# Start addresses of the tiles: a wider constant below, a small pool above

## The chip, the cores and the metric

The kernel runs on one core of a Trainium2 chip. The metric is the device time of one execution in microseconds; the kernel before has a median of 2309.77 us in three runs (2309.41 to 2312.48).

## The reference

One layer of a transformer-like trunk in float32, for 512 tokens of width 2048. The input `x` is normalised (RMS), scaled and shifted by values that a conditioning vector `c` gives through a 2048 x 12288 matrix, and projected to 7168 columns. Half of the heads (8 of width 128) run a gated linear recurrence, half (8 of width 128) run stick-breaking attention with normalised queries and keys. Their normalised outputs are concatenated, projected back to 2048 and added to `x` with a gate. Then a second normalisation of the same kind, and a feed-forward part of width 5632, `silu(gate) * up`, whose output is added with another gate:

```python
h = rms_norm(x, norm1_g[layer]) * (1.0 + sc1) + sh1
proj = h @ w_in[layer]
...
mixed = jnp.concatenate([o_hg, o_sb], axis=-1).astype(x.dtype) @ w_out[layer]
x = x + g1 * mixed

h = rms_norm(x, norm2_g[layer]) * (1.0 + sc2) + sh2
gate, up = jnp.split(h @ w_ffn_in[layer], 2, axis=-1)
x = x + g2 * ((jax.nn.silu(gate) * up) @ w_ffn_out[layer])
```

## The kernel before, in words

**Numbers.** The big products are made of matmuls in `float32r` (fp32r): each float32 operand is split into a rounded part and its remainder, and three matmuls (`hi*hi`, `hi*lo`, `lo*hi`) add up in PSUM. `three` (L227), `product` (L908) and `multiply` issue them. `split` (L212) makes the two parts of a loaded weight block: ScalarE (ACT) casts it to `hi` (L220), VectorE (DVE) subtracts to get `lo` (L221). A few small products (attention scores, transposes) are plain float32, which TensorE (PE) runs in two passes.

**Stages, in order of time.** First projection of the 1024 columns of the recurrence's values (to about 101 us; 16 blocks of rows, 24 matmuls of 512 columns each, while the rows of the conditioning matrix are read and multiplied on DVE, L180). Projections of the eight attention heads (to 445 us; 192 matmuls of 384 columns a head), with the attention of the heads before beside them. Projections of the eight recurrent heads (to 770 us; 144 matmuls of 512 columns a head), with their recurrence beside them. Output projection (to 945 us; 48 matmuls of 512 columns for each of 15 blocks, and the last block in two halves of 256). The first two blocks of the feed-forward part, 384 matmuls of 256 columns (to 1020 us). Then the loop over blocks `f` = 2 to 43 (to about 1850 us): seven products of a Strassen-like scheme on half-blocks, of 24 matmuls with 256 columns each, 168 in an `f`. In it the stationary operand (the weights) comes from `split`, the moving one is a fixed half-block of the activations, opA, opB, opC or opD. Last the output of the feed-forward part (to the end): 12 units of seven products, over 4 or 3 pairs of rows; a product has 6 matmuls of 512 columns for each pair of rows. The pairs of all units add up to 44.

The order of the instructions is written out ahead: a small clock in the kernel (`Clock`) hands out side work at planned times, and the tile framework orders the rest by priority. It inserts all waits. All large DMAs are issued from SP.

**Where tiles lie.** Each partition of the on-chip memory (SBUF) is filled from two ends. Pools with `side="right"` hang from the upper end downwards; the others stand on the lower end upwards, in the order in which they are opened; a tile takes a slot rounded up to 32 bytes. Below the first pool lie 384 bytes of the framework's own (256 of DMA scratch and four constants of 32), and above the uppermost tile 32 bytes of the 229,376 remain unused.

The lowest pool, `const`, holds small tiles for the whole run. Its slots are `cond` 8192, `small` 640, `ones` 512, `epsb` 32, `lead` 32, `mod` 384, `gain1` 64, `gain2` 64, `rcol` 32, `ident2` 512, `qkg` 32, `ba` 64, `lbt` 32, `oml` 32, `lbs` 32: 10,656 bytes. With the 384 below, the pool `wp` above it starts at byte 11,040, which is 86 x 128 + 32. Nearly all other tiles on the left have sizes that are multiples of 128, so the weights' raw blocks and their parts `hi` and `lo` (pool `wp`, L212), the activations `hhi`, `hlo`, `ohi`, `olo` (pool `hp`, L256) and opA to opD all start 32 bytes past a multiple of 128. `cond`, at byte 384, and `ones` start at one. On the right, everything ends at byte 229,344, which is 1791 x 128 + 96, and the tiles there have sizes that are multiples of 128: `xo` and `x1`, `O`, `forms`, `fhi`, `sg`, `up`, `ffS` and the spare parts `hi2` and `lo2` start 96 bytes past one. In the feed-forward loop every fourth call of `split` puts its two parts into `hi2` and `lo2` (`spare_here`, L1095) in place of `wp`; they show as `ff_2hi`, `ff_2lo` in the profile, the others as `ff_1h`, `ff_1l`. In the last stage the spare parts lie in a free piece of `opsB`, on the left.

`epsb` (L158) is a constant bias that one kind of instruction reads (L940, twice). `lead` (L160) takes two partial sums at the very start (L291, L293).

Of the kernel before, what the change touches and what calls it, by code (L numbers as in the profile page):

```python
# [10 lines left out]
F32 = mybir.dt.float32  # L11
# [6 lines left out]
P = 128  # L18
# [17 lines left out]
EPS = 1e-6  # L36
# [93 lines left out]
def trunk(ctx, tc, a):  # L130
    nc = tc.nc
    V, S, G = nc.vector, nc.scalar, nc.gpsimd
# [2 lines left out]

    const = ctx.enter_context(tc.tile_pool(name="const", bufs=1))
    wp = ctx.enter_context(tc.tile_pool(name="wp", bufs=3))
    xctx = ctx.enter_context(ExitStack())
    xop = xctx.enter_context(tc.tile_pool(name="xop", bufs=1, side="right"))
    hp = ctx.enter_context(tc.tile_pool(name="hp", bufs=1))  # L140
# [14 lines left out]
    ones = const.tile([P, P], F32, name="ones")  # L155
    G.memset(ones, 1.0)
    one = ones[:, 0:1]
    epsb = const.tile([P, 1], F32, name="epsb")  # L158
    G.memset(epsb, EPS)
    lead = const.tile([P, 2], F32, name="lead")  # L160
    left = [KT] * 6
    mod = const.tile([P, 96], F32, name="mod")
    gain1 = const.tile([P, KT], F32, name="gain1")
# [1179 lines left out]
```

## Time and profile before

| | |
|---|---|
| median of three runs | 2309.77 us |
| the profiled execution | 2309.45 us, of which the span is 2307.6 us |
| PE, DVE, ACT busy | 2253.1, 1919.5, 1160.1 us |
| mean granted TensorE clock | 0.995 of 2.4 GHz |
| DMA | 437.69 MB, 190 GB/s on the mean |

The span reaches from the first to the last instruction; the profiled execution's own time has 1.85 us more around it. Busy PE includes matmuls that overlap, so PE's share does not tell how fast they follow each other; the distance between the starts of two of them does.

### The profile page before, as it was taken

Reading aid. Unit: us, or ns where it says so; the run is one execution under the profiler, and the core shown is the slowest. Engines: PE = TensorE matmul, PEld = TensorE weight load, DVE = VectorE, ACT = ScalarE, POOL = GpSimd, SP = SyncE. Lnnn points to the kernel's source line nnn. Section 1 sums busy time; section 2 is a strip of 40 time slices with the busy share of each in tenths; the row PEclk is TensorE's granted clock in tenths of the full one; section 3 lists DMA queues with packets and bytes.
Section 4 is the critical chain, followed back from the end, with each engine's and each line's share of the span. In section 5 each row is a group of like instructions: output and inputs, shape, how many; then the busy total and the mean of one; then the engine's idle time right before and its main releaser. Section 6 shows DMA issues by size and latency. Waiting matters only on the chain.

```text
span 2307.6 us, 35720 instructions
## 1 busy us (share of the span) xinstructions
PE 2253.1 (98%) x14171; PEld 2049.8 (89%) x14171; DVE 1919.5 (83%) x2570; ACT 1160.1 (50%) x2011; POOL 10.7 (0%) x25
## 2 busy tenths in 40 slices
PE   8999899999999999989999999999999999999998
PEld 6899799888888788989999999999999978878776
DVE  8887779999887864699899988888888777888888
ACT  4326666565656422654445444454545545454443
POOL 0000000000000000000000000000000000000000
PEclk9999999999999999999999999999999999999999
DMA  9886446843322486336555534454544486654553
GB/s 368 314 319 225 166 153 230 305 170 126 110 92 76 155 294 209 111 114 238 206 203 197 209 133 165 142 174 142 174 142 157 177 343 237 219 178 142 183 204 87
DMA packets 114978, 437.69 MB, mean 190 GB/s; under 512 B 9822, under 2 KB 58236, under 8 KB 76796
## 3 DMA queue, kind: packets, MB, share of 16 engines
q1 hardware_dynamic: 114812, 435.42, 53.0%
q8 instruction: 111, 1.82, 0.3%
q14 instruction: 55, 0.45, 0.1%
HBM read 386.61 MB, written 48.77 MB: 189 GB/s over the span
## 4 chain that ended last, share of the span: by engine, by line
PE 79%; DVE 11%; DMA 4%; ACT 3%; issue 3%; SPq 0%; DVEq 0%; ACTq 0%
PE ffA L93 17%; PE ffC L93 9%; PE foA L93 8%; PE sbp L93 8%; PE wo L93 7%; PE ffB L93 4%; PE foC L93 4%; PE st L93 4%; PE hgf L93 4%; PE hgq L93 3%; PE hgg L93 3%; PE foB L93 1%; DVE ada L180 1%; PE l L93 1%; DMA opd<-fhi 1%
## 5 line engine op out<-in xcount | busy, mean ns | idle before, releaser
L180 DVE SCALAR_TENSOR_TENSOR ada<-ada,cond 128x2048 f32<-128x2048 f32 x95 | 216.9, 2286 | 49.0 <-DMA ada<-in_w_ada 49.0
L93 PE MATMUL ffA<-opD,ff_3h 128*128 128x256 f32 x512 | 93.6, 283 | 0.8 <-ACT u L1008 0.8
L93 PE MATMUL ffA<-opB,ff_6h 128*128 128x256 f32 x512 | 93.6, 283 | 0.2 <-ACT a L1008 0.2
L93 PE MATMUL ffC<-opB,ff_7h 128*128 128x256 f32 x512 | 93.5, 283 | 0.0
L93 PE MATMUL ffC<-opC,ff_4h 128*128 128x256 f32 x496 | 90.8, 284 | 0.4 <-ACT c L1008 0.3
L93 PE MATMUL ffB<-opA,ff_2h 128*128 128x256 f32 x496 | 91.3, 284 | 0.0
L93 PE MATMUL ffA<-opC,ff_5h 128*128 128x256 f32 x496 | 90.6, 283 | 0.0
L93 PE MATMUL ffA<-opA,ff_1h 128*128 128x256 f32 x496 | 90.6, 283 | 0.0
L1082 ACT CAST fhi<-forms 128x512 fp32r<-128x512 f32 (+1 forms) x63 | 43.6, 692 | 90.6 <-DMA opd<-fhi 74.1
L93 PEld LDWEIGHTS ffA<-opD,ff_3h 128*128 128x128 f32 x512 | 79.8, 192 | 1.0 <-ACT u L1008 1.0
L93 PEld LDWEIGHTS ffA<-opB,ff_6h 128*128 128x128 f32 x512 | 79.7, 192 | 0.4 <-ACT a L1008 0.4
L93 PEld LDWEIGHTS ffC<-opB,ff_7h 128*128 128x128 f32 x512 | 79.8, 192 | 0.0
L93 PEld LDWEIGHTS ffC<-opC,ff_4h 128*128 128x128 f32 x496 | 77.2, 192 | 0.8 <-ACT c L1008 0.8
L93 PEld LDWEIGHTS ffB<-opA,ff_2h 128*128 128x128 f32 x496 | 77.7, 193 | 0.1
L93 PEld LDWEIGHTS ffA<-opC,ff_5h 128*128 128x128 f32 x496 | 77.3, 192 | 0.0
L93 PEld LDWEIGHTS ffA<-opA,ff_1h 128*128 128x128 f32 x496 | 77.3, 192 | 0.0
L1083 DVE TENSOR_TENSOR forms<-forms,fhi 128x512 fp32r<-128x512 f32 (+1 forms) x63 | 49.0, 778 | 31.0 <-ACT fhi L1082 30.6
L93 PE MATMUL ffA<-opD,ff_3l 128*128 128x256 f32 x256 | 72.5, 283 | 0.0
L93 PE MATMUL ffC<-opB,ff_7l 128*128 128x256 f32 x256 | 72.4, 283 | 0.0
L93 PE MATMUL ffA<-opB,ff_6l 128*128 128x256 f32 x256 | 72.4, 283 | 0.0
L93 PE MATMUL ffB<-opA,ff_2l 128*128 128x256 f32 x248 | 70.3, 284 | 0.0
L93 PE MATMUL ffA<-opA,ff_1l 128*128 128x256 f32 x248 | 70.2, 283 | 0.0
(1644 smaller groups left out, 7759.3 us busy)
## 6 DMA issues: line engine op xcount, KB each, us to landing
ada<-in_w_ada SPq DMA_DIRECT2D x95, 1024.0 KB, 5.0
wfo<-in_w_fo SPq DMA_DIRECT2D x16, 1024.0 KB, 6.0
yraw<-in_w_fo SPq DMA_DIRECT2D x16, 1024.0 KB, 5.1
fix<-in_w_fix SPq DMA_DIRECT2D x14, 1024.0 KB, 5.7
opsA<-opd SPq DMA_DIRECT2D x12, 1024.0 KB, 4.9
opd<-forms SPq DMA_DIRECT2D x44, 256.0 KB, 3.7
opd<-fhi SPq DMA_DIRECT2D x42, 256.0 KB, 4.2
opd<-forms SPq DMA_DIRECT2D x22, 384.0 KB, 6.7
```

Source lines behind the costliest of these rows:

```text
L93: self.engine.matmul(out, lhsT, rhs, **kw)
L180: V.scalar_tensor_tensor(w, w, 1.0, row, op0=ALU.mult, op1=ALU.mult, accum_out=col)
L1082: S.copy(hi, R[:, q])
L1083: V.tensor_sub(R[:, q].bitcast(F32R), R[:, q], hi.bitcast(F32))
```

## The change

Two constant tiles are made larger, and one of them moves to a new pool that is opened first on the right side. `lead` grows from 2 to 34 columns (32 to 160 bytes of slot); only its first two are used as before. `epsb`, which had a slot of 32 bytes in `const`, becomes the first column of `epsw`, 24 columns (96 bytes), at the upper end. So `const` takes 96 bytes more in sum, all that lies above it on the left moves up by 96 bytes, to 11,136 = 87 x 128, and all that hangs below `epsw` on the right moves down by 96 bytes, to end at 229,248 = 1791 x 128. Within `const` the small tiles behind `lead` move too, and not all of them to a multiple of 128.

```diff
     wp = ctx.enter_context(tc.tile_pool(name="wp", bufs=3))
+    edge = ctx.enter_context(tc.tile_pool(name="edge", bufs=1, side="right"))
     xctx = ctx.enter_context(ExitStack())
...
-    epsb = const.tile([P, 1], F32, name="epsb")
-    G.memset(epsb, EPS)
-    lead = const.tile([P, 2], F32, name="lead")
+    epsw = edge.tile([P, 24], F32, name="epsw")
+    G.memset(epsw, EPS)
+    epsb = epsw[:, 0:1]
+    lead = const.tile([P, 34], F32, name="lead")
```

## Rows read from the trace of the kernel before

**Rows 1.** The page's busy time, share of the span and instructions, by engine.

```profile
PE 2253.1 (98%) x14171; PEld 2049.8 (89%) x14171; DVE 1919.5 (83%) x2570; ACT 1160.1 (50%) x2011; POOL 10.7 (0%) x25
```

**Rows 2.** The page's chain that ended last, by engine.

```profile
PE 79%; DVE 11%; DMA 4%; ACT 3%; issue 3%; SPq 0%; DVEq 0%; ACTq 0%
```

**Rows 3.** Busy time by stage: from:to, length, engines, granted clock, DMA share, GB/s.

```profile
12.00:101.00 89.00, 89.00 (x383) 73.20 (x383) 79.51 (x115) 38.16 (x52) 0.00 (x0) 1.00 0.95 356
101.00:445.00 344.00, 333.37 (x1930) 318.17 (x1929) 283.13 (x383) 183.75 (x448) 0.00 (x0) 0.99 0.63 229
445.00:770.00 325.00, 321.23 (x1644) 269.62 (x1642) 283.74 (x534) 198.01 (x431) 9.05 (x16) 1.00 0.35 127
...
945.00:1020.00 75.00, 68.41 (x535) 67.23 (x534) 69.77 (x160) 54.86 (x122) 0.00 (x0) 0.95 0.29 102
1020.00:1310.00 290.00, 287.54 (x2425) 286.93 (x2424) 268.10 (x304) 143.90 (x212) 0.00 (x0) 1.00 0.58 206
1310.00:1850.00 540.00, 539.56 (x4558) 539.15 (x4557) 443.23 (x503) 270.16 (x393) 0.00 (x0) 1.00 0.46 160
```

**Rows 4.** Timeline of PE in the feed-forward loop: start, length, line, out<-moving,weights, count.

```profile
1833.01 0.40 PE L93 MATMUL ffA<-opA,ff_1h 128*128 128x256 f32 x2
1833.25 0.28 PE L93 MATMUL ffA<-opA,ff_1l 128*128 128x256 f32 x1
1833.37 0.39 PE L93 MATMUL ffB<-opA,ff_2hi 128*128 128x256 f32 x2
1833.60 0.28 PE L93 MATMUL ffB<-opA,ff_2lo 128*128 128x256 f32 x1
1833.71 0.39 PE L93 MATMUL ffB<-opA,ff_2hi 128*128 128x256 f32 x2
```

**Rows 5.** Chain of waits in the last stage, then PE's timeline at 150 us.

```profile
1915.71 5.44 PE foC L93 x24
...
149.78 0.33 PE L93 MATMUL sbp<-wsb_2l,hhi 128*128 128x384 f32 x1
...
150.30 0.33 PE L93 MATMUL sbp<-wsb_2l,hhi 128*128 128x384 f32 x1
```

**Rows 6.** Plain fp32 passes: chain at 510 us; instructions by tile, with ns min/median/max.

```profile
509.82 0.86 PE r L93 x4
...
L93 PE MATMUL r<-QB_w,KB_w x32: 377/378/382, 509.7 to 793.2; 128*128 128x256 f32 x32
...
L93 PE MATMUL ssum<-ss,ones x4: 377/377/378, 947.0 to 954.0; 128*128 128x256 f32 x4
```

**Rows 7.** Timeline of POOL at the start.

```profile
0.73 0.20 POOL L156 MEMSET ones<- 128x128 f32 x1 [0.29 <-POOLq L1332]
0.87 0.10 POOL L159 MEMSET epsb<- 128x1 f32 x1
```

**Rows 8.** Instructions on `cond` and on `fhi`: count, ns min/median/max, start, forms.

```profile
L1082 ACT CAST cond<-forms x3: 612/613/827, 1867.9 to 1869.1; 128x512 fp32r<-128x512 f32 x2, 128x768 fp32r<-128x768 f32 x1
L1083 DVE TENSOR_TENSOR forms<-forms,cond x3: 684/684/951, 1869.1 to 1870.6; 128x512 fp32r<-128x512 f32 x2, 128x768 fp32r<-128x768 f32 x1
...
L1082 ACT CAST fhi<-forms x63: 618/622/841, 1033.8 to 1828.1; 128x512 fp32r<-128x512 f32 x42, 128x768 fp32r<-128x768 f32 x21
L1083 DVE TENSOR_TENSOR forms<-forms,fhi x63: 685/693/953, 1037.7 to 1828.7; 128x512 fp32r<-128x512 f32 x42, 128x768 fp32r<-128x768 f32 x21
```

**Rows 9.** Costliest groups by form, matmuls of the loop: count, busy us, mean ns.

```profile
L93 PE MATMUL ffA<-opB,ff_6h 128*128 128x256 f32 x512 | 93.6, 283 | 0.2 <-ACT a L1008 0.2
...
L93 PE MATMUL ffA<-opD,ff_3h 128*128 128x256 f32 x512 | 93.6, 283 | 0.8 <-ACT u L1008 0.8
...
L93 PE MATMUL ffB<-opA,ff_2hi 128*128 128x256 f32 x176 | 30.5, 276 | 0.0
L93 PE MATMUL ffB<-opA,ff_2lo 128*128 128x256 f32 x88 | 24.3, 276 | 0.0
L93 PE MATMUL ffA<-opD,ff_3hi 128*128 128x256 f32 x160 | 27.9, 277 | 1.4 <-ACT u L1008 1.4
L93 PE MATMUL ffC<-opB,ff_7lo 128*128 128x256 f32 x80 | 22.1, 276 | 0.0
```

## The prediction

> **What bounds the kernel now.** I read the table of engines first: PE is busy 98% of the span, DVE 83%, ACT 50% [rows 1]. The chain of waits agrees: 79% of what ended last is PE [rows 2]. Then I cut the span into its stages [rows 3]. The reader is to see two things there. The granted clock is 0.95 to 1.00 in all of them, so PE runs at its 2.4 GHz level and the clock has nothing to give. And the stages differ in what stands right behind PE: from 12 to 101 us the DMA share is 0.95; from 945 to 1020 and from 1020 to 1310 DVE is busy 93% and 92% (69.77 of 75, 268.10 of 290); from 445 to 770 87%; from 1310 to 1850 only 82%, and there PE has 539.56 of 540 us.
>
> So the time is the number of matmuls times their spacing, and the spacing is where a change of addresses could act. At 2.4 GHz 256 columns need 106.7 ns, 384 need 160.0, 512 need 213.3. The timeline shows more. In the feed-forward loop the product with `ff_1h`, `ff_1l` takes 0.36 us for three matmuls (1833.01 to 1833.37), 120.0 ns each, while the next one, with `ff_2hi`, `ff_2lo`, takes 0.34 us (1833.37 to 1833.71), 113.3 ns each [rows 4]. 24 matmuls of 512 columns take 5.44 us, 226.7 ns each; three of 384 take 0.52 us, 173.3 each [rows 5]. In cycles the excess is 32 for 256, 384 and 512 columns alike, and 16 where the weights are `hi2`/`lo2`. It is not a price of issuing: passes of plain fp32, which read each column at half the rate, follow each other at 215 ns (0.86 us for four) for 512 cycles = 213.3 ns, an excess of 1.7 ns, and are recorded as 377 to 378 ns whether their weights start at a multiple of 128 bytes (`ones`) or 32 past one (`KB_w`) [rows 6].
>
> What is different about `ff_2hi`? The moving operand is the same tile, opA. The weights lie in `hi2`/`lo2`, which hang from the right end; those of `ff_1h` lie in `wp` on the left. Adding up the tiles of the kernel text, every large tile on the left starts at 32 bytes past a multiple of 128, every one on the right at 96. Moving operands are always on the left. So rows 4 compare weights at 32 with weights at 96, both against moving data at 32, and the place of a tile is worth 16 cycles, 6.7 ns, of a matmul.
>
> **The change, part by part.** (1) `epsw` is 24 wide instead of 1: a memset of one column takes 0.10 us, one of 128 columns 0.20 [rows 7]; POOL has nothing else to do then, and the reader of `epsb` comes at 950 us. Cost 0; if it were not covered, under 0.1. (2) `lead` is 34 wide, with the same two columns used: 0. No instruction, wait or DMA is added, removed or moved; both sides have the room.
> (3) Left tiles move from 32 to 0, right ones from 96 to 0. For ACT and DVE the trace has both kinds of place: the cast of 128x512 takes 612 to 613 ns into `cond`, which already starts at a multiple of 128, and 618 to 622 into `fhi` at 96; the subtraction 684 against 685 to 693 [rows 8]. That is 0 to 1.4%. DVE's 1919.5 us would shrink by under 27, of which only the stages that DVE presses could use any: 0 to 2 us. I take 0, the nearest pairs being the minima, which differ by 1 to 6 ns. For DMA no row compares two places cleanly. It decides nothing but the first stage (DMA share 0.95, 89 us); a tenth of its transfer time lost would be 8 us there, and a gain is worth no more than the 2.6 us by which PE, busy for all 89, could be quicker (below). I take 0, and 2.6 gained and 8 lost as ends.
> (4) The matmuls. The code has 13,176 in fp32r: 384 in the first projection, 1536 in the attention projections, 1152 in the recurrent heads', 816 in the output projection, 384 in the first two feed-forward rows, 42 x 168 = 7056 in the loop, 44 x 42 = 1848 in the last product. Weights in `hi2`/`lo2` have 4 x (176 + 88) + 3 x (160 + 80) = 1776 of them, all in the loop [rows 9]; 11,400 pay 32 cycles.
>
> No row shows an operand at 0, so the price after is unknown. Its ends: a spacing with the 1.7 ns of rows 6 alone, or one that loses nothing and puts the 1776 at 32 cycles as well. I read the 32 as two terms of 16, since 16 cycles is 64 bytes of one row. One is a piece of 64 bytes that a moving row starting in the middle of such a piece reads in addition: 16 cycles whatever the length, as seen, and hidden at half rate, as seen. The other comes from the weights, loaded while the matmul before streams: both start in the same half of 128 bytes (32 and 32) and one gives way once; with 96 and 32 they don't meet. After the change the first term goes everywhere. The second stays for the 11,400, since 0 and 0 are the same half again, and comes to the 1776, which lose one term and gain the other. So 272 cycles for all: 6.7 ns off 11,400 matmuls and nothing off the rest. I choose this value because it lies next to the one row that shows an escape, 113.3 ns.
>
> **The sum**, in us, gross and what I keep: first projection 2.6, kept 0 (DMA share 0.95 is next); attention projections 10.2, kept 8 (DVE 82%, with waits of the heads between); recurrent heads 7.7, kept 5 (the heads' chains of DVE and ACT pace part of it); output projection 5.4, kept 5; first feed-forward rows 2.6, kept 1 (DVE 93%); the loop 35.2, by time 12.3 before 1310, where DVE would come to 268 of 278, kept 8, and 22.9 after, kept whole (DVE 443 of 517); last product 12.3, kept 10. Gross 76, kept 60. From the profiled execution's 2309.45 (span 2307.6; the runs' median is 2309.77, so no correction) this gives 2250. With nothing held back it is 2234; with only the output projection and the late loop kept (28) it is 2281: the forecast's own range.
>
> **Rivals.**
> *Both terms go.* If weights and moving data at 0 no longer disturb each other, the spacing falls to N/2.4 + 1.7: 11.6 ns off 11,400 and 4.9 off 1776, gross 141. Then DVE is the engine that is late: before 1310 I keep 13 of 24 (290 to 277 against DVE's 268), after it 42 of 46, elsewhere 0 + 13 + 8 + 8 + 1 + 16: 101 together, 2208. For it: the 1.7 ns of rows 6 show that issuing as such costs little. Against: nothing shows the weights' term to be one of absolute place. The Trainium skill, TensorE: Matmul & The Clock Gate, section Back-to-back issue gap, gives 262 cycles for 256 columns and 518 for 512 with a warm clock; by it the gross gain would be an estimated 131 us. The trace's fp32r matmuls don't show that spacing anywhere.
> *Only the distance counts (slower).* Place: the feed-forward loop. Mechanism: the whole excess comes from weights and moving data running at the same distance modulo 128; `hi2`/`lo2` are quicker only because they are 64 bytes off. The change makes all distances 0, the 11,400 stay at 288 cycles and the 1776 rise to 288: 1776 x 6.7 ns = 11.9 us, with PE at 539.56 of 540 nothing hides it: 2321. It decides if no matmul gets quicker by starting at 0. For it: one mechanism explains both spacings. Against: it gives no reason why exactly half remains at a distance of 64.
> *The place doesn't count.* `hi2`/`lo2` lie at the upper end of the partition and are single buffers; if one of these makes them quick, all stays: 2309, 2305 to 2314. Against: opB and opD lie some 98,000 bytes apart, and yet with `wp` weights both have the same recorded length of 283 ns, and with the spares both have 276 to 277 [rows 9]. The Trainium skill, SBUF — State Buffer, section Specifications (TRN2), states lines of 16 bytes; 32 and 96 are both multiples of that, so by that rule no tile crosses a line less than before and nothing changes. The two spacings of rows 4 speak against the rule as the whole story.
>
> **How the numbers follow.** Forecast 0.35, both terms go 0.27, only the distance counts 0.19, place doesn't count 0.16, something else 0.03 (half slower). Faster by over 0.2% (4.6 us, about what a measurement of this kernel tells from no change): 0.35 + 0.27 = 0.62; within it 0.17; slower 0.21. The cases have both signs, so the range takes in the slower one: 2195 to 2322, leaving out the lower part of the rival that gains most (0.08) and the rest.
>
> **What would show it.** Three matmuls of the loop with `wp` weights: 0.34 us if I am right, 0.325 if both terms go, 0.36 if neither. Those with `hi2`/`lo2`: 0.34, 0.325, and 0.36 in the slower case. Three of 512 columns: 0.66 us. ACT and DVE means should stay within 1.4%, DVE's share before 1310 should pass 95%, and DVE rather than PE should end more of PE's waits there. I am wrong at the root if `hi2` and `wp` weights keep 113.3 and 120.0; wrong in the division into two terms if `wp` weights go below 113 or stay at 120 while `hi2` rises.

## The result, and the profile after

The change made the kernel slower: 2318.63 us median of five runs (2317.34 to 2320.07) against 2311.02 for the kernel before in five runs of the same comparison, a ratio of 1.0034, 95% interval 1.0021 to 1.0046. The profiled execution took 2320.07 us, with a span of 2318.1.

The first fence is the profile page's table of engines and its chain of waits by engine, for the kernel after; they answer to [rows 1] and [rows 2].

```profile
PE 2265.5 (98%) x14171; PEld 2063.0 (89%) x14171; DVE 1921.2 (83%) x2570; ACT 1161.9 (50%) x2011; POOL 10.8 (0%) x25
PE 80%; DVE 12%; ACT 3%; issue 3%; DMA 2%; SPq 0%; DVEq 0%; ACTq 0%
```

PE alone grew, by 12.4 us; DVE and ACT by 1.7 and 1.8. The next fence has three stages of the kernel after, with the columns of [rows 3]: from:to, length, PE, PEld, DVE, ACT, POOL, granted clock, DMA share, GB/s.

```profile
445.00:770.00 325.00, 321.94 (x1648) 270.49 (x1646) 284.00 (x536) 198.18 (x430) 9.06 (x16) 1.00 0.35 127
...
1020.00:1310.00 290.00, 288.93 (x2406) 288.53 (x2405) 266.51 (x303) 142.76 (x210) 0.00 (x0) 1.00 0.57 203
1310.00:1850.00 540.00, 540.00 (x4502) 540.00 (x4501) 441.72 (x499) 269.42 (x390) 0.00 (x0) 1.00 0.45 155
```

In the feed-forward loop PE is busy without a gap and starts fewer matmuls in the same time: 4502 where there were 4558 between 1310 and 1850 us, at the same granted clock of 1.00. The timeline of PE in that loop says which ones are late. Each row below is the first of a product of 24 matmuls; the second product has `hi2`/`lo2` as its weights.

```profile
1701.69 0.40 PE L93 MATMUL ffB<-opA,ff_2h 128*128 128x256 f32 x2
...
1704.57 0.40 PE L93 MATMUL ffA<-opB,ff_6hi 128*128 128x256 f32 x2
...
1707.45 0.40 PE L93 MATMUL ffC<-opB,ff_7h 128*128 128x256 f32 x2
...
1710.33 0.40 PE L93 MATMUL ffA<-opC,ff_5h 128*128 128x256 f32 x2
```

All three take 2.88 us, 120.0 ns a matmul. In [rows 4] the `hi2`/`lo2` ones had 113.3. Their recorded length shows it too, 283 ns in the groups by form of the kernel after, where [rows 9] have 276:

```profile
L93 PE MATMUL ffB<-opA,ff_2hi 128*128 128x256 f32 x176 | 32.2, 283 | 0.0
...
L93 PE MATMUL ffB<-opA,ff_2lo 128*128 128x256 f32 x88 | 24.9, 283 | 0.0
```

From the starts of all matmuls of the loop its length, from the first start to the last, can be divided exactly: 7055 x 106.7 ns = 752.5 us for the columns, what the spacing has above that (the *excess*, of steps with less than 60 cycles of it), and the excess of the longer steps. Those are PE's waits with the slow step behind each, and the steps at the lower level of the clock at the start of the loop.

```
us                  loop    columns   excess, wp weights   excess, hi2/lo2   longer steps
before              842.0   752.5     70.1                 11.8              7.6
after               851.1   752.5     70.2                 23.4              5.0
```

So the 1776 matmuls with `hi2`/`lo2` went from 16 to 32 cycles of excess and cost 11.6 us; the longer steps gave 2.6 back; the other 5280 did not move. Of the longer steps 3.1 us before and 3.4 after are no waits: PE had waited 6.2 us for ACT, and its first matmuls of the loop ran at 1.2 GHz (granted clock 0.51 from 1008.0 to 1014.2 us before, 0.50 from 1008.0 to 1014.5 after). The mean of 0.95 for that stage in [rows 3] hides this stretch, which is much the same in both. The rest, waits and the slow steps behind them, fell from 4.5 to 1.6 us.

The other stages hold the rest of the 10.5 us by which the span grew: +2.1 in the attention projections, +0.8 in the last stage, between -1.1 and 0 elsewhere. The 2.1 can't be laid to the change: in the ten runs below and above whose places are equal in that stage it takes 336.2 to 338.4 us, and experiment 3, whose left side lies as in the change, has 336.2.

### The profile page after: what moved, and what is told of

Read it like the earlier page. It is cut to its first block, busy times and chain, and to the rows that moved or that the text cites. A ratio compares the mean times of both kernels' runs of the same rounds, so it can differ in the third digit from the quotient of the medians.

```text
span 2318.1 us, 35720 instructions
## 1 busy us (share of the span) xinstructions
PE 2265.5 (98%) x14171; PEld 2063.0 (89%) x14171; DVE 1921.2 (83%) x2570; ACT 1161.9 (50%) x2011; POOL 10.8 (0%) x25
## 4 chain that ended last, share of the span: by engine, by line
PE 80%; DVE 12%; ACT 3%; issue 3%; DMA 2%; SPq 0%; DVEq 0%; ACTq 0%
PE ffA L93 19%; PE ffC L93 9%; PE foA L93 9%; PE wo L93 7%; PE sbp L93 7%; PE ffB L93 5%; PE foC L93 4%; PE hgf L93 4%; PE st L93 4%; PE hgq L93 3%; PE hgg L93 3%; PE foB L93 1%; DVE ada L182 1%; PE l L93 1%; PE hgo L93 1%
## 5 line engine op out<-in xcount | busy, mean ns | idle before, releaser
L93 PE MATMUL ffA<-opC,ff_5l 128*128 128x256 f32 x248 | 70.2, 283 | 0.0
```

What stands on the lines that cost most here:

```text
L93: self.engine.matmul(out, lhsT, rhs, **kw)
```

## Experiments

In all of them a *distance* is the start of the stationary operand minus that of the moving one, modulo 256 bytes; a *spacing* is the mean step from one matmul's start to the next inside a product, and its excess is in cycles of 2.4 GHz above the number of columns. Edits are against the kernel before unless another is named. Where one execution was timed and no interval can be given, the text says "one run" and goes by the loop in its trace.

**1. Both operands moved, the pairs equal.** `lead` alone grows, so that the whole left side starts at 224 modulo 256, where `hi2`/`lo2` already lie.

```diff
-    lead = const.tile([P, 2], F32, name="lead")
+    lead = const.tile([P, 56], F32, name="lead")
```

> Only the left side moves, by 192 bytes: weights in wp and the moving operands both start 96 bytes past a multiple of 128, as the spares on the right do (distance 0 modulo 512). Theory 'distance' (the excess depends on where the weights start relative to the moving operand): wp weights stay at 120.0 ns for 256 columns and the spares rise from 113.3 to 120.0; time about +8 us, 2317 to 2321. Theory 'own place' (weights at 96 are quick, at 0 and 32 slow): spares stay at 113.3 and wp weights fall to 113.3; 512 columns 226.7 to 220; time about -60 us, 2250. Theory 'size of the constants or the end of the partition': nothing moves, 2309 to 2312.

2319.26 us, ratio 1.0032 (1.0020 to 1.0043). Starts of products in the loop, from PE's timeline of this run:

```profile
1701.62 0.40 PE L93 MATMUL ffB<-opA,ff_2h 128*128 128x256 f32 x2
...
1704.50 0.40 PE L93 MATMUL ffA<-opB,ff_6hi 128*128 128x256 f32 x2
...
1707.38 0.40 PE L93 MATMUL ffC<-opB,ff_7h 128*128 128x256 f32 x2
```

2.88 us for both kinds. Nothing of `hi2`/`lo2` itself was touched, and yet they lost their 113.3 ns: what counts is where the weights lie against the moving operand. And with equal places 120.0 ns stands at 32, 128 and 224 alike, so none of these starts costs anything by itself.

**2 and 3. Half the change each.** First the right side moves as in the change and the left stays; then the left side moves by 96 bytes and the right stays. Both make the distance of `hi2`/`lo2` 96, from 192 before and 0 in the change.

```diff
 # right side only: the change, but
+    lead = const.tile([P, 16], F32, name="lead")
 # left side only
+    lead = const.tile([P, 32], F32, name="lead")
```

> Half of the change: the right side moves down by 96 bytes, the left stays at 32. Spares start at 0, moving operands at 32: distance 96 modulo 512. 'Distance': the spares are not at 120.0; if the excess shrinks by one cycle for each 4 bytes of distance, 8 cycles remain, 110.0 ns, and the time is 6 us less, 2304; if only the half of 128 bytes counts, 113.3 or 120.0 and 2310 or 2319. 'Own place': spares at 0 are slow, 120.0, time +8 us, 2319. wp weights stay at 120.0 in all.

> The other half of the change: the left side at 128 modulo 256 as after the change, the right at 224 as before. wp weights 120.0 and 512 columns 226.7 in every theory. 'Pair of places': the spares (224 against 128) are not at 113.3; with the 25.6 cycles that the other half alone measured, 117.3, 2315. 'Own place' would keep them at 113.3, 2311.

2315.11 us, ratio 1.0018 (1.0007 to 1.0029), and 2314.90, ratio 1.0019 (1.0010 to 1.0028). PE's timeline of the first:

```profile
1701.44 0.40 PE L93 MATMUL ffA<-opB,ff_6hi 128*128 128x256 f32 x2
...
1704.26 0.40 PE L93 MATMUL ffC<-opB,ff_7h 128*128 128x256 f32 x2
...
1707.13 0.40 PE L93 MATMUL ffA<-opC,ff_5h 128*128 128x256 f32 x2
```

2.82 us with `hi2` (117.4 ns) and 2.87 with `wp` (120.0). The second, with only the left side moved:

```profile
1701.49 0.40 PE L93 MATMUL ffA<-opB,ff_6hi 128*128 128x256 f32 x2
...
1704.31 0.40 PE L93 MATMUL ffC<-opB,ff_7h 128*128 128x256 f32 x2
```

Again 2.82 us. Two edits with nothing in common but the distance have the same spacing, the same excess in the loop (18.5 us for `hi2`/`lo2`, 88.6 in all) and the same time. Each half costs about half.

**4. The left side at a multiple of 256.** `lead` with 64 columns: all `wp` weights and moving operands start at 0 modulo 256.

> The left side stands at multiples of 256 (the change has it at 128 modulo 256); the right stays at 224. 'Alignment would help if it were to 256 bytes': wp weights below 120, 512 columns below 226.7, time 2200 to 2290. 'Pair of places': equal places again, 120.0, 173.3 and 226.7; the spares (224 against 0) between 113.3 and 120.0; time 2309 to 2320.

One run, 2314.19 us. `wp` weights keep 120.0 ns, rows of 384 and 512 columns 173.3 and 226.7. Alignment buys nothing at 256 either. `hi2`/`lo2`, now at a distance of 224, have 116.8.

**5 and 6. A map inside `wp`.** The slots of the `hi` and `lo` parts are 64 or 32 bytes longer, so that the three buffers start at different places (`[P, 1024 + 16]` or `[P, 1024 + 8]` in place of `[P, 1024]`, with the same columns used).

> Each of the six buffers of wp's hi and lo is 64 bytes longer, so they stand at distances 128, 192, 256 (hi) and 320, 384, 448 (lo) from the moving operands of the loop, modulo 512, and the spares at 320. 'Distance modulo 128': 120.0 at 128, 256, 384 and 113.3 at 192, 320, 448 and for the spares; time about 25 us less than before, 2285. 'Distance with a longer period': other values at 128 and 256, down to 108.4 where the streams don't meet at all; time 2220 to 2280. 'Own place': same as modulo 128 here, since the moving operands stand at 32 modulo 128.

> As before, but 32 bytes longer each: weights at 32, 64, 96 (hi) and 0, 32, 64 (lo) modulo 128, moving operands and spares at 96. Distances modulo 512: 320, 352, 384; 416, 448, 480; spares 0. 'Distance modulo 128': 113.3 at 320 and 448, 120.0 at 384 and for the spares; 352, 416 and 480 between or beside these (linear: 110.0 at 352 and 480, 116.7 at 416). 'Own place': 113.3 at 384 and for the spares, 120.0 at 320, 416 and 448. Time 2270 to 2300 either way.

One run each, 2317.01 and 2324.10 us, far from the 2285 and the 2270 to 2300 expected. In the first the `wp` products of the loop got quicker, 116.7 to 117.9 ns, `hi2`/`lo2` at a distance of 64 had 113.5, and the loop took 839.3 us in place of 842.0. But `hi` and `lo` of a product lay at different distances, which mixes the readings, and the other stages lost more: 512 columns had excesses of 40 to 46 cycles where equal places have 32. No `wp` product had 113.3. In the second `hi2`/`lo2`, by this map at a distance of 0, rose to 119.5 ns, though they had not moved; the loop took 842.2 us, and the longer rows cost more than in the first.

**7 to 10. One distance for all of `wp`.** A small tile between `wp` and the activations moves only the moving operands of the loop (the stationary ones of the first stages), by 64, 128, 256 or 320 bytes.

```diff
+    mid = ctx.enter_context(tc.tile_pool(name="mid", bufs=1))
+    mid.tile([P, 16], F32, name="mid")    # 32, 64, 80 columns in the others
```

> A tile of 64 bytes that nothing uses stands between wp and the activations; all the weights of wp are at distance -64 (448 modulo 512) from the moving operands of the loop, in the stages where the roles are swapped at +64; the spares at 128. 'Distance, modulo 128': wp weights 113.3 ns for 256 columns (16 cycles over), 220 for 512, 166.7 for 384, spares 120.0; time about -60 us, 2250. 'Distance, longer period': wp weights between 108.4 and 120, spares not 120. If the mixing of two distances in one product is what raised the 512-column spacing of the two maps, 512 columns are at 220 or 226.7 here and not above.

> Gap of 128 bytes: wp weights at distance 384 (swapped roles: 128), spares at 64. 'Modulo 128': wp weights 120.0, spares 113.3, 512 columns 226.7, time as before, 2309 to 2313. 'Longer period': wp weights below 120, and the time lower by up to 100 us.

> Gap of 256 bytes: wp weights at distance 256 either way, spares at 448. 'Modulo 128': wp weights 120.0, spares 113.3, time as before. 'Longer period' of 512: 256 is as far as two streams can be from one another; if any distance frees them wholly it is this: 108.4 ns, 512 columns 215, time 2200 to 2230.

> Gap of 320 bytes: wp weights at distance 192, as the spares had it in the kernel before; swapped roles at 320; spares at 384. Both readings: wp weights 113.3 ns for 256 columns in the loop, which is 35 us less there; 'modulo 128' gives 120.0 for the spares and 220 for 512 columns, time 2250; where 512 columns stay at 226.7, 2285.

One run each: 2321.19, 2322.76, 2311.26 and 2318.56 us. By the loop's steps:

```
moved by       wp: distance, ns   hi2/lo2: distance, ns   512 columns, excess   loop us
0 (before)     0     120.0        192   113.3             32                    842.0
64             192   117.8        128   118.8             37 and 48             840.4
128            128   118.8        64    113.4             46 and 48             837.9
256            0     120.0        192   113.3             32                    842.3
320            192   117.8        128   118.9             37 and 48             839.5
```

The two values for 512 columns belong to stages with the weights as stationary operand and stages with the activations as such, where the distance has the other sign. Moved by 256 everything is as before, by 320 as by 64: the pattern repeats with 256 bytes; the 128 and the 512 that the expectations offered don't fit. Unequal places make the 256 columns with `wp` weights quicker and longer rows slower, so that all but the run moved by 256 are slower in sum. And one thing did not fit: at 192 the weights in `wp` have 117.8 ns and those in `hi2`/`lo2` 113.3.

**11. The same pair for both.** `lead` with 56 columns and the tile of 16 columns: `wp` starts at 224 and the moving operands at 32, exactly the pair of `hi2`/`lo2` in the kernel before. The addresses of `hi2`/`lo2` and of the moving operands are, byte for byte, those of the run moved by 256, where a product with `hi` took 2.72 us:

```profile
1698.67 0.39 PE L93 MATMUL ffA<-opB,ff_6hi 128*128 128x256 f32 x2
...
1701.39 0.40 PE L93 MATMUL ffC<-opB,ff_7h 128*128 128x256 f32 x2
```

> wp moves up by 192 bytes and a gap of 64 follows, so its weights stand at 224 modulo 256 and the activations stay at 32: the pair of places that the spares had before. 'Pair of places modulo 256': wp weights fall to 113.3 ns in the loop, 35 us gross there, 25 to 35 kept; 512 and 384 columns have an unequal pair, which so far always gave 35 to 48 cycles over against 32, so they cost 5 to 40 us more: time 2275 to 2315. 'Region or number of buffers' (the spares are quick as such): wp weights do not reach 113.3, time 2315 to 2330.

2319.75 us, ratio 1.0036 (1.0022 to 1.0051). PE's timeline:

```profile
1115.13 0.50 PE L93 MATMUL ffA<-opD,ff_3h 128*128 128x256 f32 x2 [0.80 <-ACT u L1010]
...
1117.96 0.39 PE L93 MATMUL ffA<-opA,ff_1h 128*128 128x256 f32 x2
...
1120.68 0.39 PE L93 MATMUL ffB<-opA,ff_2hi 128*128 128x256 f32 x2
...
1702.58 0.40 PE L93 MATMUL ffA<-opB,ff_6hi 128*128 128x256 f32 x2
...
1705.40 0.40 PE L93 MATMUL ffC<-opB,ff_7h 128*128 128x256 f32 x2
...
1708.23 0.40 PE L93 MATMUL ffA<-opC,ff_5h 128*128 128x256 f32 x2
```

Both kinds take 2.82 to 2.83 us, so `hi2`/`lo2` lost the 113.3 ns with neither operand moved. The time lies in what was expected if the upper region or the single buffers made them quick (2315 to 2330); but they have both of these here too, and are slow. Yet just after 1117 us, behind a wait of PE (in brackets), two products ran at 113.3, 2.72 us from 1117.96 to 1120.68 for the one with `wp` weights. So one pair of places has two steady spacings. The kernel before shows the same where PE had waited: the product with `hi2` takes 2.93 us there, in place of 2.72. About 0.11 us of that is its first step, which is slow behind any wait; the rest is the other spacing, 27 cycles of excess in place of 16.

```profile
1150.57 0.50 PE L93 MATMUL ffA<-opD,ff_3hi 128*128 128x256 f32 x2 [1.43 <-ACT u L1008]
...
1153.50 0.40 PE L93 MATMUL ffA<-opA,ff_1h 128*128 128x256 f32 x2
```

That left a theory to try: at a distance of 192 the spacing depends on what ran just before. Straight behind a product at distance 0 it is 113.3; and whichever it is, it stays until PE waits.

**12 and 13. Products at distance 0 put between the others.** Only in the loop the moving operands start 64 bytes (run 12) or 192 bytes (run 13) later inside slots that are 256 bytes longer, so that other stages keep distance 0. In run 12 the right side also ends 128 bytes lower. So `hi2`/`lo2`, every fourth product, are at 0, and the products with `wp` weights at 192 (run 12) or 64 (run 13).

```diff
+    edge = ctx.enter_context(tc.tile_pool(name="edge", bufs=1, side="right"))
+    edge.tile([P, 32], F32, name="pad")
...
+    def roomy(pool, tag, name, k, off):
+        t = pool.tile([P, k * T + 64], F32R, tag=tag, name=name)
+        return t[:, off:off + k * T]
...
-    early = fh.tile([P, 2, HALF, 2, HT], F32R, tag="b1", name="opA")
+    early = roomy(fh, "b1", "opA", KT, 16).rearrange("p (g j h t) -> p g j h t", g=2, j=HALF, h=2)
 # opB, opC, opD the same; hhi and hlo with off=0; run 13: off=48 and no edge
```

> Against the kernel before. Only the loop's moving operands opA to opD start 64 bytes later in their slots, and the right side ends 128 bytes lower, so that in the loop the products with wp weights have a distance of 192 bytes modulo 256 and those with hi2/lo2, every fourth, a distance of 0. All other stages keep distance 0. Theory R (the spacing at 192 depends on what ran before: entered straight from a product at distance 0 it is 272 cycles, entered from elsewhere 282.6, and it stays so until PE stalls): wp products at 113.3 ns, hi2/lo2 at 120.0; the mean falls from 118.3 to 115.0 ns, 7056 x 3.33 = 23.5 us gross, of which 15 after 1310 us stay and 2 to 6 before it: 2289 to 2295 us. Rival S (the steady 117.8 ns that wp weights showed at the same pair of places in the run with wp at 224 belongs to wp or to the pair): wp products 117.8, hi2/lo2 120.0, mean 118.3: 2309 to 2313 us.

> As the run before, but opA to opD start 192 bytes later in their slots and the right side stays: wp weights at a distance of 64, hi2/lo2 at 0. Theory R, with 64 as good as 192: the same 2289 to 2295 us, 113.3 and 120.0 ns. If 64 gives its low spacing to the upper region alone (there it was 113.3 once): about 117.8 and 120.0, 2309 to 2313.

Run 12: 2308.53 us, ratio 0.9989 (0.9980 to 0.9998). Run 13: 2310.93, ratio 0.9999 (0.9990 to 1.0009). PE's timeline of run 12:

```profile
1640.05 0.40 PE L93 MATMUL ffC<-opB,ff_7hi 128*128 128x256 f32 x2
...
1642.93 0.39 PE L93 MATMUL ffA<-opC,ff_5h 128*128 128x256 f32 x2
...
1645.65 0.39 PE L93 MATMUL ffC<-opC,ff_4h 128*128 128x256 f32 x2
...
1648.37 0.39 PE L93 MATMUL ffA<-opD,ff_3h 128*128 128x256 f32 x2
...
1651.09 0.40 PE L93 MATMUL ffA<-opA,ff_1hi 128*128 128x256 f32 x2
```

2.88 us with `hi2`, and then three products with `wp` weights at 2.72 us, 113.3 ns: the first time that `wp` weights had it in a steady stretch. The roles are exchanged against [rows 4]. Stretches of the loops show the rule. Each number is the mean excess of one product in cycles, S marks `hi2`/`lo2`, a bar stands where PE had waited; the slow first step behind a wait adds about 11 to a mean, so that `|27` is a product at 16, `|38` one at 27 and `|42` one at 32:

```
before    32 32 16S 32 32 32 |38S 31 32 32 16S 32 32 32 16S
run 11    27 |27 16 16S |38 27 |38 27S 27 27 27 27S 27
run 12    |42S 16 16 16 32S |38 27 27 31S 16 16 16 |41S |38 27 27 31S 16 16 16 32S 16 16 16 32S
run 13    |29 16 32S 27 27 27 32S 27 27 27 32S
```

Behind a wait the products at 192 mostly run at 27 cycles (15 of 18 times in run 12; three times at 16), and mostly the next product at 0 sets them back to 16. Of 220 `wp` products in run 12, 167 had 16. For a distance of 64 the rule is another: behind 0 it gives 27, but behind a wait 16, all four times (run 13), and behind 128 it gave 16 (the run moved by 128).

But the time missed the 2289 to 2295 that I had expected. The view of waits says where: PE's waits for other engines in the loop of run 12 (us in total, times, longest).

```profile
PE ffA L93 <- ACT u L1015: 5.6, 4, 2.1
PE ffA L93 <- ACT b L1015: 3.1, 5, 1.2
PE ffC L93 <- ACT c L1015: 2.3, 6, 0.6
```

These are the taps, ACT's copies out of an accumulator that the next product on it needs: 11.0 us in sum, 2.7 in the kernel before. With shorter products they come too late, and most of these waits also cost the low spacing. Excess fell from 81.9 to 63.0 us, the longer steps rose from 7.6 to 22.3, and the loop kept 4.2 of 18.9 us. Of the 22.3 us 3.9 are steps at 1.2 GHz: at the loop's start, as before, and once more from 1152.4 to 1155.8 us (granted clock 0.51), behind a wait of PE of 2.14 us.

**14. Every eighth product at distance 0.** Run 12 with one count changed in the loop.

```diff
-        if spare and count[0] % 4 == 0:
+        if spare and count[0] % every[0] == 0:      # 8 in the loop, 4 after it
```

> As the first of these runs (wp at 192, hi2/lo2 at 0), but only every eighth product of the loop takes hi2/lo2. Theory R: the low spacing holds through seven products: mean 114.2 ns, 0.8 ns x 7056 = 6 us gross less than the first run, less what products lose that follow a stall of PE and wait for the next one at distance 0 (up to 22 cycles each matmul, seven products at most, some ten stalls: up to 4 us; and less lead in the buffers): 2285 to 2296 us. If the low spacing decays after a few products: no better than the first run, wp products in part at 117.8.

2300.93 us, ratio 0.9957 (0.9943 to 0.9971): faster than the kernel before and the changed one, but not the 2285 to 2296 expected. PE's timeline, a product with `hi` at distance 0 and the seven at 192 that follow it:

```profile
1781.37 0.40 PE L93 MATMUL ffA<-opD,ff_3hi 128*128 128x256 f32 x2
...
1784.25 0.39 PE L93 MATMUL ffA<-opA,ff_1h 128*128 128x256 f32 x2
...
1786.97 0.39 PE L93 MATMUL ffB<-opA,ff_2h 128*128 128x256 f32 x2
...
1800.57 0.39 PE L93 MATMUL ffA<-opD,ff_3h 128*128 128x256 f32 x2
...
1803.29 0.40 PE L93 MATMUL ffA<-opA,ff_1hi 128*128 128x256 f32 x2
```

2.72 us for the first, and 2.72 for the seventh: the low spacing does not fade by itself. In the loop the excess is 60.8 us, the longer steps 20.1, the whole 833.4 (842.0 before). Of 257 `wp` products 169 had 16 cycles; most of the others had 27, behind a wait and until a product at 0 set them back. The chain of waits of its profile page shows the bound begin to pass to DVE and the DMAs, 17% and 6% where [rows 2] have 11% and 4%:

```profile
PE 69%; DVE 17%; DMA 6%; issue 4%; ACT 3%; SPq 0%; DVEq 0%; ACTq 0%
```

**15. Longer rows.** The `wp` buffers of both parts start so that, until 770 us, blocks of 24 matmuls follow each other at distances 0, 64 and 192 in turn. The edit gives the slots of `hi` 64 and of `lo` 128 bytes more and an offset of 0 or 64 bytes by the buffer's number, with a tile of 48 columns above `wp`.

> Against the kernel before. The wp buffers of hi and lo get different starts, so that until 770 us the blocks of 24 matmuls follow each other at distances 0, 64 and 192 in turn (384 and 512 columns); later stages mix distances and are not read. Theory R carried over to longer rows: in the attention projections and in the recurrent heads' two of three blocks at N + 16 cycles, 6.7 ns x 1024 = 6.8 us and 6.7 x 768 = 5.1 us less in these two stages, before stalls. Rival: longer rows have no low spacing: 384 columns near 35 cycles and 512 columns at 37 and 48 at distances 192 and 64, whatever runs before: 1 us and 3 to 4 us longer in these stages.

One run, 2324.11 us. PE's timeline in the first stage, one row a block: `wi8` at 192, `wi9` at 0, `wi10` at 64.

```profile
57.83 0.39 PE L93 MATMUL st<-wi8h,hhi 128*128 128x512 f32 x1
...
63.33 0.39 PE L93 MATMUL st<-wi9h,hhi 128*128 128x512 f32 x1
...
68.78 0.39 PE L93 MATMUL st<-wi10h,hhi 128*128 128x512 f32 x1
...
74.38 0.39 PE L93 MATMUL st<-wi11h,hhi 128*128 128x512 f32 x1
```

5.50, 5.45 and 5.60 us for 24 matmuls: excesses of 38, 33 and 48 cycles. For 512 columns equal places are the best of the three, and a block at 0 ahead doesn't help. Rows of 384 columns have 31.5 to 32 at 64 and 192 here and 33.4 to 34.5 at 0; without blocks at 0 between them, they had 34 to 37 on the mean at 64 (runs 7, 10 and 11), so what ran before may count there too; no run settles it. The low spacing of 16 was seen with the loop's 256 columns alone. The attention projections took 334.7 us (336.3 before, 336.2 to 338.4 in all runs with equal places there), the recurrent heads' 333.1 (330.1).

## Why the prediction was wrong

**What bounds the kernel** was read rightly: matmuls times their spacing, in the loop with nothing to hide a change. The small terms held too: the two wider tiles cost nothing that shows, and for ACT and DVE the start of a tile makes no difference that shows. In the kernel after the instructions of [rows 8] have these counts and minimum, median and maximum in ns:

```profile
L1084 ACT CAST fhi<-forms x63: 618/621/837, 1034.8 to 1836.4; 128x512 fp32r<-128x512 f32 x42, 128x768 fp32r<-128x768 f32 x21
L1085 DVE TENSOR_TENSOR forms<-forms,fhi x63: 682/693/953, 1038.7 to 1837.1; 128x512 fp32r<-128x512 f32 x42, 128x768 fp32r<-128x768 f32 x21
```

The medians are 621 and 693 where they were 622 and 693, now at a multiple of 128; the 1% by which `cond` is quicker isn't its alignment. The first stage, where DMAs press, went from 89.9 to 88.8 us, in the bounds of that term. That the clock has nothing to give missed the 3.1 us at the start of the loop, which the change doesn't touch.

**The step that failed** is in part (4): "I read the 32 as two terms of 16", one of them from a moving row that starts in the middle of a piece of 64 bytes, which "goes everywhere". There is no such term. At moving starts of 0, 32, 128 and 224 modulo 256 the spacing at distance 0 is 120.0 ns (the kernels before and after, experiments 1 and 4), whether the start is the middle of a piece of 64 bytes (32, 224) or its beginning (0, 128). So the 76 us of gross gain were never there, and the 60 kept fell with them. The other half of the reading, a clash between weights and moving row that depends on where one lies against the other, was real, and it holds the whole excess that places can change. The prediction had named the sign of this: `wp` staying at 120 while `hi2` rises.

**The rival that came true** is *Only the distance counts*, given 0.19. It said 2321, with 1776 x 6.7 = 11.9 us and nothing to hide it. Measured: 11.6 us of excess, 2.6 of them against longer steps, since PE waits less when the loop is slower; 9.1 us in the loop of the profiled executions, 7.6 between the medians. The stated range, 2195 to 2322, holds the measured 2318.63 only because it took in this rival; the way that the time would go was called wrongly, with 0.62 for faster. Two of its details were wrong. The distance counts modulo 256, not 128. And a distance alone doesn't give the spacing: the argument held against it, that it "gives no reason why exactly half remains", had a ground. At 192 there is a spacing of 16 cycles and one of 27, and the kernel before got the 16 because three products at distance 0 ran ahead of each one with `hi2`/`lo2`. That the 16 was half of 32 was what led to two terms; it is one of several values (16, 24, 26, 27, 29).

*Both terms go* fell with the first term. By the gap of 262 cycles that the Trainium skill states for an isolated matmul (TensorE: Matmul & The Clock Gate, section Back-to-back issue gap) the spacing for 256 columns would be an estimated 109 ns; the lowest steady one of fp32r in any run here is 272 cycles, 113.3. *The place doesn't count* fell with experiment 1: there `hi2`/`lo2` stay where they are, at the upper end and single, and lose their advantage. The lines of 16 bytes that the Trainium skill states (SBUF — State Buffer, section Specifications (TRN2)) explain none of it, since every start of a matmul's operand in these runs is a multiple of 32 bytes.

**What stays open.** The runs show a dependence on the distance, on the columns and on what ran before. They don't show the mechanism: two streams that meet at fixed offsets and settle into one of several rhythms would look like this, but nothing here looks inside. Why 64 takes its low spacing behind 128 and not behind 0, and why a wait of PE takes the low spacing from 192 most times and gives it to 64, wasn't settled.

## What to carry to other kernels

If two groups of like matmuls differ in spacing, compare the *difference* of their operands' starts before the starts themselves, and move one operand alone to find out: a change that aligns everything makes all differences equal, which here was the worst case for 256 columns and the best for 512. Where a spacing is exact over many instructions, divide a stage into columns, excess and longer steps before and after; a gain in excess that comes back as waits (18.9 us became 4.2) shows the next bound at once. An even fraction in a measured excess is no evidence for that many causes.

## What the runs showed that was not expected

- The spacing of fp32r matmuls with 256 columns has memory. At a distance of 192 the same addresses ran at 113.3 ns behind a product at distance 0, at 117.8 behind others, and kept the low one through seven products (19 us); it changed mostly where PE waited. A wait of PE of 1.43 us thus cost the product behind it another 0.2 us (2.93 in place of 2.72), half of it in its slow first step.
- In steady stretches: distance 0 gives 32 cycles for 256 and 512 columns and 32 to 35 for 384; for 256 columns 96 gives 26, 128 gives 29, 224 gives 24, and 64 and 192 give 16 or 27; 512 columns have 37 to 38 at 192, 46 to 48 at 128 and 48 at 64.
- Inside a product at such a distance the steps form a pattern that repeats, as 25, 32, 25, 20, 27 cycles at 96 (experiment 2), while at 0 each step is 32 once it has settled.
